# Folding the fourth quarter of the odd layer's weights in the opening instead of in the second attention

## The chip, the cores and the metric

The kernel is one launch on one NeuronCore of a Trainium2 chip. Its metric is the device time in microseconds (us) of that core. The engines named below are PE (TensorE, the matrix engine; PEld is its weight load), DVE (VectorE), ACT (ScalarE), POOL (GpSimd) and SP (SyncE, which here only issues DMA transfers). They run side by side, each works through its own instructions in order, and semaphores make one wait for another.

## The reference: what is computed

One step of a two-layer model on 1024 latent and 256 context tokens of width 1024, all in float32. Layer 0 is attention: mixer A is global, mixer B reads a band of 128 tokens to either side, and both also read the context. Layer 1, the odd layer, mixes by a Fourier transform over positions and over the channels of a group:

```python
def fourier_mix(u):
    b, s, _ = u.shape
    ug = u.astype(jnp.float32).reshape(b, s, C_GROUPS, C_GROUP_DIM)   # 4 groups of 256
    f = jnp.fft.fft2(ug, axes=(1, 3), norm="ortho")
    return jnp.real(f).reshape(b, s, C_WIDTH).astype(u.dtype)

def odd_mix(h, w_in, w_out):
    u, gate = jnp.split(h @ w_in, 2, axis=-1)
    return (fourier_mix(u) * jax.nn.silu(gate)) @ w_out
```

The transform over the channels of a group is linear and follows `h @ w_in` directly, so a kernel may apply it to the weights: for each of the four groups the 1024 x 256 block of `w_in` is multiplied once by a 256 x 256 table of cosines and sines. That product is called the fold here, one group's share of it a quarter.

## The kernel before

Products that need float32 accuracy are mostly made of three cheaper ones: each operand is split into a rounded high part (type fp32r) and the rest, and high*high, high*low and low*high are summed. The fold itself multiplies plain float32.

**The fold.** `fold_load` (L586) brings the table (`fch`, tile `h`, 256 KB) if it isn't there, and the quarter's weights in two transfers of 512 KB (`w<-i_wuT`, L592) into two buffers of zone `w`, which has eight. `fold_piece` (L603) makes a fourth of a quarter: four matrix products into one PSUM bank (`wa`, L609), of which the profile counts two instructions each, then a copy out of PSUM by ACT (L316). A quarter is thus 32 matmul instructions and four ACT copies. Its result goes to DRAM (`wd`, L599) and is read again in the odd layer (L1607), at about 940 to 990 us.

**Where quarters are folded.** Quarters 0 to 2 are folded first of all: the string `PH0` (L32) is the opening's list of steps, and its order is the order in which SP issues the opening's transfers (L709 fixes that order for SP; on the other engines a scheduler orders the instructions). `f0 f1 f2` are the loads, `F00` to `F23` the pieces, whose results wait in pairs in `u` buffers, and `G00` to `G21` the six stores of 512 KB, which stand later in the list. Of the other steps, `x0`, `x1` and `x2` load the tokens, `L0` to `L3` and `A0` to `A3` load and multiply the modulation weights (`ada`), `M` turns such a product into shift and scale (`modt`, then DVE's `modb` and `moda`), `T`, `X`, `Y` transpose and modulate the tokens, and `K`, `R` multiply them by the first projection (`kv0s` to `kv6s`). `ADA_BEHIND` (L59) holds a part of the `ada` products back until a named matmul stands ahead of them; its first entry names quarter 2's last piece.

Quarter 3 is done some 690 us later. Attention runs over units (one query block of 128 tokens, one key/value head, two query heads), and a queue of other matrix work, the filler (L97), is let out between units, by a credit per unit: first the projections of gate, query and key, then `FLATE`'s quarter (four pieces, credit 1.3 each), then the output projection of layer 0 (`oz`, `proj_step` L1387, credit 7.7 a step). Only the first steps of that projection may run inside the attention (`can_run`, L1456), since they need finished rows of all heads; their inputs are brought by POOL and SP, multiplied by POOL (L1284, L1285), and split into high part (ACT, L316) and low part (DVE, L322).

**An attention unit** of mixer B takes from PE scores (`sC` for the context, `sB` for the band), transposes of the probabilities (`pt`, L1108) and the product with the values (`av`, L1114); from DVE the band's mask (L1067), the row maxima (L1023), the low part of the transposed probabilities (L1111) and the sum of two halves (L1125); from ACT the exponentials and the copies of high parts; from SP the load of queries (`q<-qd`, L994) and the store of results.

`EF` (L41) says how many quarters are laid out in DRAM for the opening: for those, each of the two transfers holds all rows of the contraction for one half of the columns, so that two pieces can start after the first one.

```python
EF = 3
ADA_BEHIND = {(0, 0): ("wa", 2, 3), (1, 0): ("xt", 0, 2), (2, 0): ("xt", 0, 4), (2, 16): ("kc", 2, 3)}
FLATE = "f3"
```

Of the kernel before, what the change touches and what calls it, by code (L numbers as in the profile page):

```python
# [9 lines left out]
F32 = mybir.dt.float32  # L10
# [18 lines left out]
WSTEP = ((2, 1, 2), (1, 0, 1))  # L29
ORD_B = (0, 2, 3, 4, 7, 6, 5, 1, 8, 9)  # L30
AT_K, AT_Q, AT_X, NX1, GL = 1, 2, 5, 7, 3
PH0 = """f0 f1 f2 x0 S0 N0 L0 F00 F01 F02 F03 w0 L1 F10 F11 F12 F13 F20 F21 F22 F23 x1 A0 T0 s0 M0 T1 X0 X1 T2 L2 N1 K0 K1  # L32
 A1 T3 M1 L3 X2 X3 K2 K3 Y0 R0 Y1 R1 w1 G00 G01 S1 T4 A2 x2 N2 Y2 T5 M2 R2 G10 G11 G20 G21 X4 Y3 X5 R3
 K4 Y4 K5 A3 T6 Y5 M3 R4 X6 T7 R5 X7 Y6 K6 Y7 K7 R6 R7"""
S1 = """s1 S2 V Z0 Z1 c0 I0 a2 Z2 Z3 c1 I2 a1 q0 P Z4 Z5 I4 a2 P Z6 Z7 I6 a1 q2 P a2 P k8 a2 P a3 P a9 P"""
ADA_Z = (("p", "pt", "q"),) * 4
# [1 line left out]
XZ = ("u", "u", ("p", "pt", "q"))  # L38
E_ML = ("dp", "dp", "d")
E_MF, E_MH, LC0 = "da", "d", "ppd"  # L40
EF = 3  # L41
QPRE, HOLD, AHEAD = 0, 0, 2
PLACE = (
    ((0, 0, 128),), ((128, 0, 128),), ((385, 0, 127), (256, 127, 1)), ((257, 0, 128),), ((769, 1, 127), (512, 0, 1)),
# [11 lines left out]
WARM = 3  # L56
STEP_BEHIND = {(0, 2, 0, 3): ("xt", 2, 3)}
LONG = ((0, 2, 1, 3), "ckt1", "kT00")
ADA_BEHIND = {(0, 0): ("wa", 2, 3), (1, 0): ("xt", 0, 2), (2, 0): ("xt", 0, 4), (2, 16): ("kc", 2, 3)}  # L59
BEHIND = {7: 5}  # L60
ROWS_BEHIND = (9,)
PW1 = "11111"
# [6 lines left out]
FILL_C, NLATE = 2.9, 8  # L69
E_FQ, E_GD = "d", "d"  # L70
ORDER = "qa0 qa1 kb0 qb0 qb1 g0 g1 g2 g3"
FLATE = "f3"
AT_B = "s"
AT_F = (0, 1, 2)
AT_N, AT_Z = (0, 0, 3, 0, 3, 2, 2, 2, 2, 2, 3, 3, 3), ("p", "pt", "q")
# [71 lines left out]
def hybrid_step(ctx: ExitStack, tc: tile.TileContext, I, O):  # L147
# [26 lines left out]
    def drop(*bufs):  # L174
        for b in bufs:
            stamp[0] += 1
            spare[b.zone].append((stamp[0], b.idx))
# [125 lines left out]
    def queue_behind(ins, first):  # L303
        tc.add_manual_dep(
            getattr(ins, "ins", ins), getattr(first, "ins", first).name,
            mybir.DependencyInfo(mybir.DependencyClass.NoSync, mybir.DependencyReason.DATA), reason="order",
        )
# [205 lines left out]
    def ada_mm(ps, j, b, raw, start, stop):  # L513
        return pe.matmul(ps[32 * j : 32 * j + 32, 0:P], csw[:, b, :], raw, start=start, stop=stop)
# [31 lines left out]
    def ada_chunk(kk, raws):  # L546
        ps = bank("g", f"ada{kk}")
        for b in range(8):
            for j in range(4):
                part, i = divmod(j, 2)  # L550
                raw = raws[b // 4 * 2 + part]
                mm = ada_mm(ps, j, b, raw[:, b % 4, i * P : i * P + P], b == 0, b == 7)
                if (kk, 4 * b + j) in ADA_BEHIND:
                    queue_behind(mm, lows[ADA_BEHIND[kk, 4 * b + j]])
        if kk == 1:
# [30 lines left out]
    def fold_load(g):  # L586
# [4 lines left out]
        for i in range(2):  # L591
            sp.dma_start(wu[i].a, I["wuT"][g, i])  # L592
        if g < EF:
            return lambda j, c: wu[c // 512][:, j * 512 + c % 512 :][:, 0:P], wu
# [8 lines left out]
    def fold_piece(g, kb2, wu, first=False):  # L603
# [22 lines left out]
        if kb2 == 3:  # L626
            drop(*wu[1])
            fold["n"] = fold.get("n", 0) + 1
            if fold["n"] in (EF, 4):
                drop(f)  # L630
# [79 lines left out]
    region.__enter__()  # L710
    for op in PH0.split():
        first_step(op)
# [743 lines left out]
    def can_run(i, j):  # L1456
        r = pairs[i][j]

        def fn():
            if sum(len(spare[z]) for z in OB[0]) < NSP or i > EARLY:  # L1460
                return False
            return all(finished.get(t, 99) + SPAN < clock[0] for t in USES[r])
        return fn
# [5 lines left out]
    def load_to(n):  # L1469
        while loaded[0] <= min(n, 9):  # L1470
            proj_load(*steps[loaded[0]])
            loaded[0] += 1
        return 0


    def late_fold(nm):
        def fn():
            ws[nm] = fold_load(int(nm[1]))
            return 0
        return fn  # L1480

    for n, nm in enumerate(FLATE.split()):
        fl_.add(0.0, late_fold(nm))
        if n == 0:
            fl_.add(0.0, lambda: load_to(0), ready=can_run(0, 0))
        for k in range(4):
            fl_.add(FC, lambda k=k, nm=nm: fold_piece(int(nm[1]), k, ws[nm]))
    if not FLATE:
        fl_.add(0.0, lambda: load_to(0), ready=can_run(0, 0))
# [571 lines left out]
```

## Time and profile before

| what | value |
|---|---|
| time before, median of three runs | 1179.93 us (1179.76 to 1182.26) |
| the profiled execution's own time | 1181.93 us |
| its span, first to last instruction | 1180.1 us |
| mean granted TensorE clock | 0.995 |
| PE, PEld, DVE, ACT, POOL busy in the span | 98%, 88%, 70%, 48%, 28% |
| quarters 0 to 2 on PE | 6.3 to 27.2 us |
| quarter 3 on PE | 690.2 to 706.3 us, in four pieces between attention units |

A timeline row reads: start, duration, engine, line, operation, output<-inputs, form, count of merged instructions, and in brackets the engine's idle time just before it with what ended it. A row of windows reads: the window, its length, busy time and count of instructions for PE, PEld, DVE, ACT and POOL, the granted clock, the share of the 16 DMA engines' time, and GB/s. Matmuls are pipelined and their recorded ends are modelled, so that a row of x8 ends later than the next row begins; the distance from start to start is what a matmul costs.

### The profile page before, as it was taken

The page shows a single profiled execution, that of the slowest core. Times are in us where ns is not written, and L with a number is a line of the kernel's source. Part 1 is how long each engine was busy: PE and PEld are TensorE (multiplying, and loading weights), DVE is VectorE, ACT ScalarE, POOL GpSimd, SP SyncE. Part 2 cuts the span into 40 slices and gives each one's busy share as a digit, 9 for nine tenths or more (in the row PEclk, how much of TensorE's full clock was granted, in tenths as well). Part 3 has the DMA queues.
Part 4 walks back from the last instruction along what each step waited for, and adds up shares of the span by engine and source line. Part 5 has one row for each costly group of instructions (what it writes and reads, how often), then busy time and mean ns, then how long its engine had stood idle before and what let it go on. Part 6 is the DMA issues. An engine that isn't in the chain of part 4 may idle for free.

```text
span 1180.1 us, 22034 instructions
## 1 busy us (share of the span) xinstructions
PE 1151.1 (98%) x8120; PEld 1035.5 (88%) x8120; DVE 829.7 (70%) x1996; ACT 570.2 (48%) x1149; POOL 329.8 (28%) x293
## 2 busy tenths in 40 slices
PE   9998999999999999999999989999999999999997
PEld 8797999999999998899989878887777889998886
DVE  3589787877777776678888877776765962468543
ACT  4343466565656655556666674432363234342211
POOL 2345733512222230010110035365221226200001
PEclk9999999999999999999999999999999999999999
DMA  9977412323532232344352587784214426364321
GB/s 368 371 275 256 129 62 68 97 83 101 151 90 79 77 97 85 94 127 117 78 154 78 158 227 211 232 238 162 90 46 143 151 98 181 100 213 146 125 107 54
DMA packets 112592, 168.80 MB, mean 143 GB/s; under 512 B 25946, under 2 KB 63574, under 8 KB 112484
## 3 DMA queue, kind: packets, MB, share of 16 engines
q1 hardware_dynamic: 109972, 158.74, 42.6%
q0 software_dynamic: 2368, 8.39, 2.4%
q8 instruction: 64, 1.05, 0.4%
q14 instruction: 44, 0.36, 0.1%
q10 hardware_dynamic: 144, 0.26, 0.1%
HBM read 123.19 MB, written 44.16 MB: 142 GB/s over the span
## 4 chain that ended last, share of the span: by engine, by line
PE 70%; DMA 13%; DVE 8%; issue 3%; POOL 2%; ACT 2%; SPq 1%; POOLq 0%; DVEq 0%; ACTq 0%
PE of L296 9%; PE av L1114 9%; PE pt L1108 8%; PE ga L296 8%; PE q L296 8%; PE sL L989 5%; PE u L296 5%; PE g1O L296 3%; PE kv L296 3%; PE sC L989 2%; PE g1E L296 2%; PE oz L296 2%; DMA u<-i_x 2%; DMA wd<-u 2%; PE g1c L296 1%
## 5 line engine op out<-in xcount | busy, mean ns | idle before, releaser
L1111 DVE TENSOR_TENSOR pt<-pt,pt 128x512 fp32r<-128x512 f32 (+1 forms) x264 | 170.9, 658 | 40.5 <-ACT pt L316 39.5
L316 ACT ACTIVATE pt<-pt 128x512 fp32r<-128x512 f32 (+1 forms) x265 | 147.5, 576 | 101.8 <-PE pt L1108 56.2
L1114 PE MATMUL av<-pt,u 128*128 128x256 f32 x1008 | 167.5, 290 | 1.4 <-DVE e L1125 0.8
L1108 PE MATMUL pt<-identr,p 128*128 128x128 f32 x1008 | 157.2, 273 | 1.5 <-ACT p L1030 0.8
L296 PE MATMUL q<-w,u 128*128 128x256 f32 x960 | 145.1, 287 | 0.5 <-ACT e L559 0.5
L1114 PEld LDWEIGHTS av<-pt,u 128*128 128x128 f32 x1008 | 139.1, 190 | 5.0 <-DVE e L1125 1.0
L296 PEld LDWEIGHTS q<-w,u 128*128 128x128 f32 x960 | 127.2, 189 | 5.5 <-ACT e L559 0.7
L1030 ACT ACTIVATE p<-p,nm 128x1280 f32<-128x1280 f32 (+1 forms) x80 | 95.4, 1193 | 68.2 <-DVE p L1023 68.0
L1108 PEld LDWEIGHTS pt<-identr,p 128*128 128x128 f32 x1008 | 119.7, 141 | 8.1 <-ACT p L1030 1.0
L296 PE MATMUL ga<-u,w 128*128 128x512 f32 (+1 forms) x576 | 124.4, 360 | 0.8 <-DVE byp L1085 0.5
L296 PEld LDWEIGHTS ga<-u,w 128*128 128x128 f32 x576 | 93.8, 188 | 15.4 <-ACT pt L316 1.2
L322 POOL TENSOR_TENSOR w<-h,w 128x512 fp32r<-128x512 f32 x38 | 50.0, 1331 | 134.6 <-DVE w L318 106.6
L989 PE MATMUL sL<-u,q 128*128 128x512 f32 x256 | 82.3, 409 | 0.0
L1030 ACT ACTIVATE p<-p,NM 128x640 f32<-128x640 f32 (+2 forms) x80 | 59.2, 740 | 31.5 <-DVE p L1023 31.2
L989 PE MATMUL sC<-u,q 128*128 128x256 f32 x320 | 62.1, 294 | 2.3 <-DMA q<-qd 2.0
L1023 DVE TENSOR_SCALAR_CACHE_REDUCE p<-sL 128x512 f32<-128x512 f32 x64 | 43.8, 685 | 22.3 <-PE sL L989 14.0
L1023 DVE TENSOR_SCALAR_CACHE_REDUCE p<-sL,nm 128x512 f32<-128x512 f32 x64 | 47.7, 745 | 13.9 <-PE sL L989 12.8
L296 PE MATMUL oz<-u,w 128*128 128x512 f32 x192 | 56.4, 399 | 0.4 <-DVE e L1125 0.4
L759 POOL TENSOR_TENSOR h<-h,rope 128x512 f32<-128x512 f32 (+1 forms) x18 | 21.6, 1199 | 121.4 <-ACT h L842 79.2
L989 PEld LDWEIGHTS sC<-u,q 128*128 128x128 f32 x320 | 48.8, 189 | 5.9 <-issue 2.6
L322 POOL TENSOR_TENSOR u<-h,u 128x512 fp32r<-128x512 f32 x16 | 21.0, 1323 | 109.1 <-ACT u L316 81.2
L296 PE MATMUL of<-u,u 128*128 128x512 f32 x150 | 48.2, 393 | 0.0
(735 smaller groups left out, 2590.7 us busy)
## 6 DMA issues: line engine op xcount, KB each, us to landing
q<-qd SPq DMA_DIRECT2D x80, 256.0 KB
h<-i_w_in SPq DMA_DIRECT2D x40, 256.0 KB
h<-i_w_out SPq DMA_DIRECT2D x32, 256.0 KB
p<-i_ada_s SPq DMA_DIRECT2D x11, 512.0 KB
qd<-pt SPq DMA_DIRECT2D x20, 256.0 KB
qd<-q SPq DMA_DIRECT2D x18, 256.0 KB
w<-i_wuT SPq DMA_DIRECT2D x8, 512.0 KB
u<-i_x SPq DMA_DIRECT2D x8, 512.0 KB
```

Source lines behind the costliest of these rows:

```text
L296: last = pe.matmul(out, a, b, start=i == 0, stop=i == n - 1)
L316: return act.activation(out, in_, AF.Copy)
L322: return pick("lo" + lc, lc).tensor_sub(dst_l, src, dst_h)
L759: pick("rope", XE["rope"]).tensor_mul(t1.rearrange("p t h (b c) -> p t (h b) c", b=2), y.rearrange("p t h (b c) -> p t (h b) c", b=2), cb)
L989: pe.matmul(ps, q_at(q, s, hc), keys, start=s == 0, stop=s == 1)
L1023: dve.tensor_scalar(p[i][:, end[i] : end[i] + n], ps, sign, last[i], op0=ALU.mult, op1=ALU.min, accum_out=c)
L1030: act.activation(p[i][:, 0 : end[i]], p[i][:, 0 : end[i]], AF.Exp, bias=last[i], scale=-1.0, accum_out=SU[:, t, hd + i, 0:1],)
L1108: pe.transpose(tp[:, jj * 256 + i * P : jj * 256 + i * P + P], p[i][:, off : off + P], ident)
L1111: dve.tensor_sub(pt[:, 1, 0:n], tp[:, 0:n], pt[:, 0, 0:n])
L1114: pe.matmul(acc, vv, pt[:, s, jj * 256 : jj * 256 + 256], start=c + jj + s == 0, stop=c + jj == nt - 1 and s == 1,)
```

## The change

Quarter 3 joins the opening. Its loads stand behind those of quarter 2, its four pieces behind quarter 2's, and its two stores behind quarter 2's. The load of the first projection's weights (`w0`, with `L1`) moves behind quarter 1's pieces, since four quarters fill the eight `w` buffers. The first modulation products now stand behind quarter 3's last piece. The filler loses quarter 3, its two loads and the second load of the table.

```diff
-PH0 = """f0 f1 f2 x0 S0 N0 L0 F00 F01 F02 F03 w0 L1 F10 F11 F12 F13 F20 F21 F22 F23 x1 A0 T0 s0 M0 T1 X0 X1 T2 L2 N1 K0 K1
- A1 T3 M1 L3 X2 X3 K2 K3 Y0 R0 Y1 R1 w1 G00 G01 S1 T4 A2 x2 N2 Y2 T5 M2 R2 G10 G11 G20 G21 X4 Y3 X5 R3
+PH0 = """f0 f1 f2 f3 x0 S0 N0 L0 F00 F01 F02 F03 F10 F11 F12 F13 w0 L1 F20 F21 F22 F23 F30 F31 F32 F33 x1 A0 T0 s0 M0 T1 X0 X1 T2 L2 N1 K0 K1
+ A1 T3 M1 L3 X2 X3 K2 K3 Y0 R0 Y1 R1 w1 G00 G01 S1 T4 A2 x2 N2 Y2 T5 M2 R2 G10 G11 G20 G21 G30 G31 X4 Y3 X5 R3
...
-EF = 3
+EF = 4
...
-ADA_BEHIND = {(0, 0): ("wa", 2, 3), (1, 0): ("xt", 0, 2), (2, 0): ("xt", 0, 4), (2, 16): ("kc", 2, 3)}
+ADA_BEHIND = {(0, 0): ("wa", 3, 3), (1, 0): ("xt", 0, 2), (2, 0): ("xt", 0, 4), (2, 16): ("kc", 2, 3)}
...
-FLATE = "f3"
+FLATE = ""
```

The scheduler then orders the engines anew. SP's queue from its first transfer on, before the change (`h<-i_fch` is the table, `w` the folded weights, `u<-i_x` the tokens):

```order
L589 DMA h_135<-i_fch 128x512
L592 DMA w_137<-i_wuT 128x1024
L592 DMA w_138<-i_wuT 128x1024
L592 DMA w_141<-i_wuT 128x1024
L592 DMA w_142<-i_wuT 128x1024
L592 DMA w_145<-i_wuT 128x1024
L592 DMA w_146<-i_wuT 128x1024
L450 DMA u_149<-i_x 128x1024
```

And of the change:

```order
L589 DMA h_135<-i_fch 128x512
L592 DMA w_137<-i_wuT 128x1024
L592 DMA w_138<-i_wuT 128x1024
L592 DMA w_141<-i_wuT 128x1024
L592 DMA w_142<-i_wuT 128x1024
L592 DMA w_145<-i_wuT 128x1024
L592 DMA w_146<-i_wuT 128x1024
L592 DMA w_149<-i_wuT 128x1024
L592 DMA w_150<-i_wuT 128x1024
L450 DMA u_153<-i_x 128x1024
```

Two transfers of 512 KB have come in ahead of the tokens and of everything behind them.

The second place is DVE in the second attention, the rows that end with the low part of the first output projection's input (`w<-u,w`, L322), without which that projection can't go beyond its first products. In names such as `sC_20` and `sB_300` the first figure (2 or 3) tells mixer B's key/value head, the second the pair of query heads, a third the head of the pair; before the change:

```order
L1023 TENSOR_SCALAR p_9496,NM<-sC_20_9497,nsink 128x256
L1081 TENSOR_REDUCE tot_9687<-SU 128x16
L1082 TENSOR_SCALAR tot_9687<-tot_9687 128x16
L1023 TENSOR_SCALAR p_9640,NM<-sC_21_9641,nsink 128x256
L1083 RECIPROCAL tot_9687<-tot_9687 128x16
L1111 TENSOR_TENSOR pt_9516<-pt_300_9511,pt_9516 128x512
L1085 COPY byp_9693<-tot_9687 128x16
L322 TENSOR_TENSOR w_9318<-u_9308,w_9317 128x1024
```

And of the change:

```order
L1125 TENSOR_TENSOR e_9445<-av_20_9431,e_9444 64x256
L1111 TENSOR_TENSOR pt_9522<-pt_302_9517,pt_9522 128x512
L1067 SCALAR_TENSOR_TENSOR p_9770<-sB_300_9778,maskf 128x384
L1067 SCALAR_TENSOR_TENSOR p_9770<-sB_301_9783,maskf 128x384
L1023 TENSOR_SCALAR p_9770,nm_301_9769<-sC_30_9771,nsink 128x256
L1081 TENSOR_REDUCE tot_9681<-SU 128x16
L1023 TENSOR_SCALAR p_9770,NM<-p_9770,nm_300_9768 128x384
L1125 TENSOR_TENSOR e_9485<-av_21_9471,e_9484 64x256
L1111 TENSOR_TENSOR pt_9532<-pt_304_9529,pt_9532 128x256
L1023 TENSOR_SCALAR p_9770,NM<-p_9770,nm_301_9769 128x384
L1082 TENSOR_SCALAR tot_9681<-tot_9681 128x16
L322 TENSOR_TENSOR w_9344<-u_9334,w_9343 128x1024
```

The next unit's masks and maxima (`sB_300`, `sB_301`, `sC_30`) now stand ahead of that low part; before they stood behind it. Counted from the last row of the gate projections (L878) up to and with the low part, DVE has 31 rows before and 41 now: six more of L1023, two more each of L1067, L1111 and L1125, and two of the small rows on `tot` fewer.

The third place is PE at the same point, the rows up to the first output projection (`oz`). Before the change, where `wa` are matmuls of quarter 3's last piece:

```order
L609 MATMUL wa_9402<-h_9298,w_9300 128x256
L609 MATMUL wa_9402<-h_9298,w_9301 128x256
L989 MATMUL sC_20_9497<-u_4487,q_9432 128x256 x2
L989 MATMUL sC_30_9704<-u_7091,q_9506 128x256 x2
L989 MATMUL sC_21_9641<-u_4487,q_9432 128x256 x2
L1108 MATMUL pt_310_9651<-identr,p_9456 128x128 x4
L1114 MATMUL av_21_9477<-pt_9483,u_4487 128x256 x4
L296 MATMUL oz_9564<-u_8516,w_9317 128x512
```

And of the change:

```order
L989 MATMUL sC_31_9815<-u_7123,q_9500 128x256 x2
L1061 MATMUL sB_310_9822<-u_7121,q_9500 128x384 x2
L1061 MATMUL sB_311_9827<-u_7121,q_9500 128x384 x2
L296 MATMUL oz_9558<-u_8548,w_9343 128x512
L296 MATMUL oz_9558<-u_8549,w_9343 128x512
L1114 MATMUL av_30_9504<-pt_9510,u_7123 128x256 x4
L1114 MATMUL av_30_9504<-pt_9522,u_7122 128x256 x4
L1114 MATMUL av_30_9504<-pt_9532,u_7122 128x256 x2
L1108 MATMUL pt_314_9669<-identr,p_9450 128x128 x2
L296 MATMUL oz_9558<-u_8548,w_9344 128x512
```

No `wa` is left there. Up to the third `oz` product, the first one that needs the low part, PE now has 8 more of `sB`, 4 more of `sC`, 6 more of `pt` and 10 more of `av` than it had before up to the first `oz`.

## The prediction

> **What bounds the kernel now.** I begin with the page's busy row and the slices of PE and of its granted clock.
>
> ```profile
> PE 1151.1 (98%) x8120; PEld 1035.5 (88%) x8120; DVE 829.7 (70%) x1996; ACT 570.2 (48%) x1149; POOL 329.8 (28%) x293
> PE   9998999999999999999999989999999999999997
> ```
>
> PE is the bound over the whole, and the change takes no matmul away: 32 of them go from one place to another. So the time moves only by what PE waits, or runs slowly, at the old and the new place. The windows view shows both places.
>
> ```profile
> 30.00:40.00 10.00, 7.77 (x108) 6.64 (x107) 5.42 (x17) 7.45 (x13) 3.09 (x3) 0.98 1.03 407
> 40.00:50.00 10.00, 10.00 (x110) 8.50 (x109) 5.56 (x9) 1.45 (x2) 4.61 (x3) 0.84 1.05 402
> 690.00:708.40 18.40, 16.16 (x105) 14.79 (x106) 16.07 (x50) 14.66 (x35) 8.59 (x9) 1.00 0.96 271
> 750.00:760.00 10.00, 8.49 (x39) 7.27 (x40) 9.66 (x27) 7.48 (x20) 0.72 (x1) 0.83 0.54 167
> ```
>
> The opening has a hole in PE (7.77 of 10 us) followed by a granted clock of 0.84, with the DMA engines full (share 1.03). The stretch with quarter 3, 690 to 708.4, is the one to look at twice: DVE is busy 16.07 of 18.40 us there and none of that is the fold's, whose copies run on ACT. Quarter 3 fills PE time that DVE would largely leave empty.
>
> **The opening.** The timeline gives the quarter's price and what PE waits for behind it.
>
> ```profile
> 6.33 20.88 PE L609 MATMUL wa<-h,w 128*128 128x256 f32 x96
> 12.48 0.33 SPq L542 DMA_DIRECT2D p<-i_ada  x1
> 13.77 0.33 SPq L542 DMA_DIRECT2D pt<-i_ada  x1
> 34.16 1.06 ACT L459 ACTIVATE h<-u 128x1024 bf16<-128x1024 f32 x1
> 36.11 0.27 PE L566 MATMUL modt<-identr,e 128*128 128x128 f32 x1
> 36.39 1.42 DVE L465 TENSOR_SCALAR u<-u,n11ry 128x1024 f32<-128x1024 f32 x2 [0.88 <-POOL n11ry L275]
> 37.98 0.16 DVE L532 TENSOR_TENSOR moda<-moda,gT 128x4 f32<-128x4 f32 x1
> 38.09 0.41 PE L471 MATMUL xt<-identr,u 128*128 128x128 f32 x2 [1.71 <-DVE moda L531]
> 39.02 0.50 PE L576 MATMUL kv0s<-w,u 128*128 128x256 f32 x2 [0.52 <-ACT u L484]
> ```
>
> 96 matmuls in 20.88 us are 0.2175 us each, so quarter 3 adds 32 x 0.2175 = 6.96 us of PE ahead of the first `ada` product. SP issues one 512 KB transfer per 13.77 - 12.48 = 1.29 us there, so everything behind the two new loads comes 2.6 us later. PE comes 7.0 us later, hence it no longer waits for what the queue brings: the 1.71 us at 38.09 ended when DVE's `moda` was made, behind the normalising of tokens (L465) that hangs on ACT's squares at 34.16 and so on the load of `x1`. That chain moves by 2.6 us, PE's arrival by 7.0. The 0.52 us at 39.02 is the same chain's next step. Both are covered: -2.2 us. The clock row at 40 to 50 shows 0.84: 10 x 0.16 = 1.6 us of PE work lost, right behind these two gaps. Without the gaps I take the loss as gone. The opening costs +6.96 - 1.71 - 0.52 - 1.6 = **+3.1 us**.
>
> Here a rule bears on the sum. TensorE: Matmul & The Clock Gate, in the Trainium skill, says under Why this matters for your kernels that the clock falls to half after PE idles for a window of about 3.4 us and advises no gaps over about 3 us. The gaps here were 1.71 and 0.52 us and the clock fell all the same, so the trace is stricter than that advice. By the rule alone these gaps wouldn't be the cause, the 1.6 us would stay, and the opening would cost +4.7.
>
> The bounds: +7.0 if nothing is covered. Below, waits further on could absorb the rest:
>
> ```profile
> PE ad L514 <- DMA p<-i_ada_s: 2.2, 2, 1.5
> PE ad L514 <- DMA q<-i_ada_s: 1.0, 1, 1.0
> 49.90 7.00 SPq L599 DMA_DIRECT2D wd<-u  x4
> 76.97 0.65 PE L514 MATMUL ad<-p,e 128*32 128x128 f32 x16
> ```
>
> The first two rows (waits from 0 to 130 us) sum to 3.2 us, so 0 is the low end. I take +3.1, since these transfers are issued late and move along with PE's work. The other queue effect is the two added stores: four took SP 7.00 us, so two take 3.5, and transfers behind them come 2.6 + 3.5 = 6.1 us later. They are the `ada_s` loads, issued from 57 us and first used at 76.97; PE's own shift and that distance hide it. The buffers that the stores release are taken up later in the list, and I price them at nothing.
>
> **The second attention.** Rows of DVE and PE around quarter 3:
>
> ```profile
> 690.12 0.69 DVE L1111 TENSOR_TENSOR pt<-pt,pt 128x512 fp32r<-128x512 f32 x1
> 690.22 1.97 PE L609 MATMUL wa<-h,w 128*128 128x256 f32 x8 [0.39 <-ACT pt L316]
> 692.06 0.47 DVE L1023 TENSOR_SCALAR_CACHE_REDUCE p<-sC,nsink 128x256 f32<-128x256 f32 x1
> 692.46 0.54 DVE L1067 SCALAR_TENSOR_TENSOR p<-sB,maskf 128x384 f32<-128x384 f32 x1
> 693.05 0.51 PE L1061 MATMUL sB<-u,q 128*128 128x384 f32 x2
> 693.41 0.52 PE L1114 MATMUL av<-pt,u 128*128 128x256 f32 x3
> 693.53 0.60 DVE L1023 TENSOR_SCALAR_CACHE_REDUCE p<-p,nm 128x384 f32<-128x384 f32 x1
> 696.21 0.40 DVE L1125 TENSOR_TENSOR e<-av,e 64x256 f32<-64x256 f32 x1
> 697.45 0.60 PE L1108 MATMUL pt<-identr,p 128*128 128x128 f32 x4
> 697.81 1.19 PE L1114 MATMUL av<-pt,u 128*128 128x256 f32 x8
> 698.84 0.38 PE L1108 MATMUL pt<-identr,p 128*128 128x128 f32 x2
> 703.02 0.48 DVE L1023 TENSOR_SCALAR_CACHE_REDUCE p<-sC,nsink 128x256 f32<-128x256 f32 x1 [1.79 <-PE sC L989]
> 704.41 1.89 PE L609 MATMUL wa<-h,w 128*128 128x256 f32 x8
> 705.41 1.23 DVE L322 TENSOR_TENSOR w<-u,w 128x1024 fp32r<-128x1024 f32 x1 [0.22 <-ACT w L316]
> 708.46 0.87 PE L296 MATMUL oz<-u,w 128*128 128x512 f32 x3
> ```
>
> Before, DVE runs 31 rows from the end of L878 at 690.12 to the end of the low part (705.41 + 1.23 = 706.64): 16.5 us, with 1.79 + 0.22 = 2.0 idle. The change puts 41 rows there. By these durations the ten are 6 x 0.53 (L1023, 0.47 to 0.60) + 2 x 0.69 + 2 x 0.54 + 2 x 0.40, less some 0.4 for two small rows: 6.0 us. Each row starts some 0.07 us before the last one ends (690.12 + 0.69 against 690.73 is typical), 0.8 over twelve: 5.2. So DVE needs 19.7 us if its idle time goes (the 1.79 was a load of queries that shared the DMA engines with the fold's traffic) and 21.7 if not. I take the middle, 20.7: the low part ends at 710.8 on the old clock of that place and the main run of `oz` starts there, against 708.46: +2.3 us. Though 7 us of matmuls are gone, the projection starts later.
>
> But PE then has less left. It has done 10 more `av` ((698.84 - 697.81) / 8 = 0.13 each), 6 `pt` ((697.81 - 697.45) / 4 = 0.09), 8 `sB` ((693.41 - 693.05) / 2 = 0.18) and 4 `sC`, which I price like `av`: 1.3 + 0.5 + 1.4 + 0.5 = 3.7 us. Net -1.4, between -2.4 and -0.4.
>
> Behind it stands a second stall:
>
> ```profile
> 750.35 0.28 PE L1088 MATMUL tt<-identr,byp 128*16 128x128 f32 x1 [0.85 <-DVE pt L1111]
> 750.95 0.33 PE L1108 MATMUL pt<-identr,p 128*128 128x128 f32 x1 [0.32 <-DVE ssp L1418]
> 752.11 0.55 PE L1108 MATMUL pt<-identr,p 128*128 128x128 f32 x3 [0.84 <-ACT p L1030]
> ```
>
> These 0.85 + 0.32 + 0.84 = 2.0 us, with the clock of 0.83 behind them (1.7 us), come from DVE being behind. With 5.2 us of its rows done earlier they may go or stay: between -3.7 and 0, and I take half, -1.9. The place gives -1.4 - 1.9 = **-3.3 us**, between -6.1 and -0.4.
>
> From there on the same work follows in a slightly other order, which the windows from 850 to 1050 bound:
>
> ```profile
> sum 200.00, PE 195.50 PEld 172.30 DVE 119.13 ACT 79.12 POOL 59.78; mean PE 48.87 PEld 43.07 DVE 29.78 ACT 19.78 POOL 14.95
> ```
>
> PE idles 4.5 of 200 us there. I take 0 for it, within 1.5 either way.
>
> **The sum.** +3.1 - 3.3 = -0.2 us on the profiled execution's 1181.93, so 1181.7. That execution stands 2.0 above the median of 1179.93, hence 1179.7 for the median. A measurement of this kernel can tell about 0.2%, 2.4 us, from no change; the forecast lies within it.
>
> **Rivals.**
>
> *The stretch gives all back (faster).* If DVE runs without idling and the stall at 750 with its clock drop goes, the place gives -6.1, and with the opening at +3.1 the time falls by 3.0 to 1176.9. For it: the DMA engines at 0.96 in that stretch lose the quarter's traffic. Against: the 41 rows in the order.
>
> *The emptied stretch drops the clock (slower).* PE's 16.16 busy us lose the fold's (1.97 + 3 x 1.89 = 7.6) and gain 3.7: 12.3 us of work in 20.7. The two clock losses above followed stretches with little PE work, so here the clock may stay at half. Then PE needs 24.6 us where DVE needs 20.7: 3.9 us more, in all 1183.6. It decides once PE's work at half clock exceeds DVE's 20.7. Against it: from 690 to 708 PE waits 2 us for queries already and the clock reads 1.00. The same page of the Trainium skill says, under PE-mode transpose, that transposes don't count as PE work for the clock; the `pt` rows here are transposes, which speaks for this rival, and no row here shows it by itself.
>
> *The opening is not covered (slower).* If PE meets its waits at 38 and 39 us again and the clock drops again, the opening costs +7.0 and the sum is +3.7, 1183.6. It decides once the `x1` chain moves by as much as PE does, 7.0 us instead of 2.6.
>
> That quarter 3 is folded twice or not at all is excluded by the order of instructions.
>
> **Chances and range.** Forecast (within 0.2%) 0.44; the stretch gives all back 0.30; clock 0.12; opening uncovered 0.14. So faster 0.30, same 0.44, slower 0.26. The forecast's own range is 1177.6 to 1182.3. For 8 in 10 I go below the first rival by a part of the opening's low end, to 1174.5, and above the slower two by a little, to 1184.5.
>
> **What would show it.** Opening: the `modt` of the second `ada` product followed by no wait of 1.7 us, the clock at 1.00 from 40 to 50 us, and the `ad` products at 76.97 some 3 us later. Attention: PE waiting for DVE between the last `ga` and the first `oz`, DVE almost without idle time there, and the third `oz` about 20 us behind the last L878. The prediction is wrong if `oz` follows within 17 us, if the clock reads below 0.9 in that stretch, or if the 1.71 us wait stays.

## The result and the profile after

| | before | after |
|---|---|---|
| time, median of four runs each | 1180.84 us (1179.76 to 1182.26) | 1194.49 us (1192.64 to 1195.88) |
| ratio | | 1.0105, 95% interval 1.0078 to 1.0132 |
| profiled execution's own time | 1181.93 us | 1195.64 us |
| its span | 1180.1 us | 1193.6 us |

The change makes the kernel 13.7 us slower, far more than the 0.2% (2.4 us) that a measurement can tell. The forecast of no change was wrong, and so was its range, which ended at 1184.5. (The ratio of the two medians alone is 1.0116, a little above the ratio given but within its interval.)

The page of the changed kernel, rows of busy time and slices:

```profile
PE 1156.5 (97%) x8120; PEld 1039.5 (87%) x8120; DVE 838.8 (70%) x1996; ACT 569.3 (48%) x1149; POOL 331.3 (28%) x293
PE   9999999999999999999999979999999998999997
```

The instruction counts are those of before. PE is busy 5.4 us longer (1156.5 against 1151.1) and idle 8.1 us longer (span less busy: 37.1 against 29.0). Slices hide this; the view of windows finds the places. First the changed kernel (window, its length, busy us and instructions of PE, PEld, DVE, ACT, POOL, granted clock, DMA share, GB/s):

```profile
30.00:40.00 10.00, 10.00 (x108) 8.49 (x106) 1.98 (x6) 5.17 (x11) 1.88 (x2) 1.00 1.00 371
40.00:50.00 10.00, 9.46 (x146) 8.07 (x145) 8.92 (x19) 6.38 (x11) 4.65 (x4) 1.00 1.02 399
65.00:80.00 15.00, 14.51 (x123) 14.10 (x122) 12.04 (x23) 8.34 (x15) 6.90 (x6) 1.00 0.95 351
612.00:625.00 13.00, 10.70 (x61) 9.45 (x59) 10.10 (x30) 9.02 (x19) 2.59 (x2) 0.87 0.73 204
690.00:712.00 22.00, 15.93 (x118) 14.84 (x116) 14.84 (x46) 11.55 (x28) 7.18 (x9) 0.89 0.87 230
973.00:1013.00 40.00, 34.26 (x266) 31.38 (x265) 9.72 (x30) 13.71 (x32) 17.75 (x22) 0.96 0.48 143
```

The same view of the kernel before, for the windows that the prediction didn't show:

```profile
65.00:80.00 15.00, 14.95 (x161) 14.38 (x161) 12.75 (x31) 5.73 (x10) 6.63 (x6) 1.00 0.54 200
612.00:625.00 13.00, 13.00 (x80) 11.51 (x79) 11.92 (x37) 9.60 (x22) 1.29 (x1) 1.00 0.58 154
690.00:712.00 22.00, 19.75 (x121) 17.73 (x122) 17.27 (x53) 15.91 (x39) 11.85 (x14) 1.00 0.92 262
973.00:1013.00 40.00, 38.58 (x365) 36.76 (x363) 11.03 (x42) 16.74 (x44) 22.02 (x25) 1.00 0.60 178
```

In the opening the hole and the lost clock at 30 to 50 are gone, but the DMA engines are at 0.95 instead of 0.54 from 65 to 80. At 612 and from 690 PE idles and loses clock, and in the Fourier mixing, at 973, PE gets through 266 instead of 365 instructions. Laid side by side by the start of the same matmul (the n-th with the same output), PE stands behind the profiled execution of before as follows. The marks are the 29th `kv4s` (66.1 us before), the `ga` at 565, the last `ga` (687), the last `oz` of layer 0 (851), the first `u` of the Fourier stage (973), the `u` at 1012 and the last `of` (1173). The first four rows fold quarter 3 late, as before. Each row is one profile. Ahead of each mark PE has done the same matmuls in all of them, except those of quarter 3. The last `modt`, at 65.3 us, would not do as a mark: the changed kernel is only 3.1 us late there, but runs 15 other matmuls behind it (3 `q`, 6 `kv0s`, 6 `kv2s`) that stood ahead of it before.

| us behind, at | 66 | 565 | 687 | 851 | 973 | 1012 | 1173 | median of the runs |
|---|---|---|---|---|---|---|---|---|
| before again (e4) | -0.7 | 1.0 | 0.6 | -0.9 | -0.9 | -0.1 | -0.1 | 1181.85, one run |
| two more stores (e8) | -0.1 | 5.3 | 4.2 | 2.6 | 2.1 | 2.2 | 2.2 | 1183.86 |
| other turn of buffers (e13) | -0.7 | -0.2 | -0.4 | -0.5 | -0.5 | 5.3 | 5.4 | 1186.72 |
| a `u` buffer, before (e14) | -0.1 | 0.7 | 0.1 | -1.1 | -1.1 | 0.6 | 0.4 | 1181.10 |
| **after** | 5.9 | 5.9 | 7.3 | 7.1 | 7.2 | 13.5 | 13.7 | 1194.49 |
| folded twice (e1) | 5.7 | 6.3 | 6.7 | 13.8 | 12.2 | 14.4 | 14.3 | 1196.07 |
| empty quarter kept (e2) | 5.9 | 7.2 | 7.3 | 12.3 | 10.6 | 12.1 | 12.0 | 1194.52 |
| late part alone (e3) | -0.2 | 2.6 | 1.0 | -2.0 | -2.3 | 2.6 | 2.5 | 1187.81 |
| no gate loads (e6) | 4.0 | 5.1 | 7.3 | 17.6 | 15.9 | 21.6 | 21.8 | 1203.89 |
| a `u` buffer (e7) | 5.3 | 5.8 | 5.6 | 5.6 | 5.6 | 7.0 | 7.1 | 1188.89 |
| stores from POOL (e9) | 5.0 | 6.0 | 8.2 | 7.8 | 7.9 | 16.6 | 16.8 | 1196.15 |
| queries ahead (e11) | 5.6 | 7.5 | 9.2 | 9.6 | 8.9 | 19.9 | 20.2 | 1198.55 |
| queue's turn (e12) | 7.2 | 7.2 | 9.2 | 10.9 | 10.7 | 16.3 | 16.5 | 1194.43 |
| no stores of quarter 3 (e15) | 4.0 | 3.0 | 4.9 | 5.6 | 5.0 | 11.4 | 11.6 | 1193.11 |

In its one repeat (e4) the kernel before stands within 1 us of its first profile at these marks; the times of its runs beside the experiments lay between 1172.87 and 1185.44. For the changed kernel the row splits into 5.9 (opening) + 1.4 (565 to 687) - 0.2 (attention and projection) + 0.1 + 6.3 (973 to 1012) + 0.2 = 13.7 us.

### The profile page after: what moved, and what is told of

It reads as the page before. It is cut to its first block, busy times and chain, and to the rows that moved or that the text cites. A ratio compares the mean times of both kernels' runs of the same rounds, so it can differ in the third digit from the quotient of the medians.

```text
span 1193.6 us, 22024 instructions
## 1 busy us (share of the span) xinstructions
PE 1156.5 (97%) x8120; PEld 1039.5 (87%) x8120; DVE 838.8 (70%) x1996; ACT 569.3 (48%) x1149; POOL 331.3 (28%) x293
## 4 chain that ended last, share of the span: by engine, by line
PE 79%; DVE 7%; DMA 6%; issue 3%; ACT 2%; POOL 1%; SPq 1%; POOLq 0%; DVEq 0%; ACTq 0%
PE av L1114 9%; PE of L296 9%; PE pt L1108 9%; PE ga L296 9%; PE q L296 8%; PE sL L989 5%; PE u L296 4%; PE oz L296 3%; PE g1O L296 3%; PE sC L989 3%; PE kv L296 3%; PE wa L609 2%; PE g1E L296 2%; PE g1c L296 1%; PE sB L1061 1%
## 5 line engine op out<-in xcount | busy, mean ns | idle before, releaser
L1111 DVE TENSOR_TENSOR pt<-pt,pt 128x512 fp32r<-128x512 f32 (+1 forms) x264 | 170.6, 658 | 39.7 <-ACT pt L316 38.9
L322 POOL TENSOR_TENSOR w<-h,w 128x512 fp32r<-128x512 f32 x38 | 50.5, 1346 | 132.2 <-DVE w L318 104.8
L296 PE MATMUL oz<-u,w 128*128 128x512 f32 x256 | 65.4, 398 | 1.9 <-DVE h L1308 1.2
L1023 DVE TENSOR_SCALAR_CACHE_REDUCE p<-sL 128x512 f32<-128x512 f32 x64 | 43.9, 686 | 23.5 <-PE sL L989 14.7
L296 PEld LDWEIGHTS oz<-u,w 128*128 128x128 f32 x256 | 47.2, 188 | 13.1 <-DVE h L1308 1.5
L1023 DVE TENSOR_SCALAR_CACHE_REDUCE p<-sL,nm 128x512 f32<-128x512 f32 x64 | 47.7, 746 | 13.0 <-PE sL L989 11.9
L322 POOL TENSOR_TENSOR u<-h,u 128x512 fp32r<-128x512 f32 x22 | 31.0, 1419 | 89.7 <-ACT u L316 89.4
```

What stands on the lines that cost most here:

```text
L296: last = pe.matmul(out, a, b, start=i == 0, stop=i == n - 1)
L322: return pick("lo" + lc, lc).tensor_sub(dst_l, src, dst_h)
L1023: dve.tensor_scalar(p[i][:, end[i] : end[i] + n], ps, sign, last[i], op0=ALU.mult, op1=ALU.min, accum_out=c)
L1111: dve.tensor_sub(pt[:, 1, 0:n], tp[:, 0:n], pt[:, 0, 0:n])
```

## The experiments

**e1, e2: is it the missing quarter?** Both start from the changed kernel. e1 folds quarter 3 at the old place as well. e2 takes and gives back the old place's buffers and lets the same credits pass, with empty pieces.

```diff
 e1
-FLATE = ""
+FLATE = "f3"
 e2
-FLATE = ""
+FLATE = "f3"
-            ws[nm] = fold_load(int(nm[1]))
+            ws[nm] = [take(z, (P, n)) for z, n in (("h", 512), ("w", 1024), ("w", 1024))]
-            fl_.add(FC, lambda k=k, nm=nm: fold_piece(int(nm[1]), k, ws[nm]))
+            fl_.add(FC, lambda k=k, nm=nm: drop(take("h", (P, 512)), *(ws[nm] if k == 3 else ())))
```

> Quarter 3 is folded twice: in the opening as after the change, and again in the second attention as before it (the same numbers are stored twice). Theory A (three separate costs: the opening some +6 us, a late weight load with a clock loss near 618 us +3 us, and the buffers in the Fourier stage near 975 to 1005 us +6.4 us, while the emptied stretch near 700 us gives nothing net): the opening's cost alone remains here, 1187 us, or 1190 us if the loss near 618 us comes along. Theory B (the opening costs the predicted +3.1 us and all the rest, some 10 us, comes from the stretch that the change empties): 1184 us.

> The changed kernel, but the filler keeps an empty quarter: at the old place the same buffers (one of zone h for the table, two of zone w, one of zone h per piece) are taken and given back with the same credits, and nothing is loaded, multiplied, copied or stored there. From the odd layer on every tile then lies in the buffers that it had before the change. Theory A (the 6.4 us lost between 975 and 1005 us come from the other buffers and the other order of loads that follows): 1188 us, no new loss between 975 and 1005 us. Theory B (they come from the shifted times, whatever the buffers): 1194 us.

e1: 1196.07 us (ratio 1.0139, interval 1.0110 to 1.0169); e2: 1194.52 us (1.0122, 1.0084 to 1.0160). Neither theory's time came in e1; e2's time is theory B's, but its loss lies where theory A had it. From 687 to 851 e1 loses 7.1 us and e2 5.0: 32 matmuls more or less at the late place are worth about 2 us, not 7. (That both lose there, though e1 does what the kernel before does, goes with the scheduler's order, which it made anew: PE's rows there differ from both kernels'.) What is new: with the old place's buffers booked, the loss from 973 to 1012 shrinks to 2.2 (e1) and 1.5 us (e2) from 6.3. The Fourier stage is sensitive to which buffers the filler took, 280 us earlier.

**e3, e8: the two halves apart.** Both start from the kernel before. e8 stores quarter 2's result twice, so that the opening has six stores but no more matmuls. e3 does the same and also leaves the late fold out; quarter 2 stands in for quarter 3.

```diff
 e3 alone
-FLATE = "f3"
+FLATE = ""
 e3 and e8
-            fold_put(i // 10, i % 10 * 512, e.a)
+            [fold_put(q, i % 10 * 512, e.a) for q in ((2, 3) if i // 10 == 2 else (i // 10,))]
```

> The kernel of before without quarter 3 in the second attention, and without it in the opening: quarter 3's place in DRAM gets quarter 2's result by two more stores, so 32 matmuls, three loads and four copies are left out. From the odd layer on the buffers and the order are those of the changed kernel. Theory A: the emptied stretch gives nothing net although 7 us of matmuls are gone, and the Fourier stage costs 6.4 us: 1187 us. Theory B (the Fourier stage's loss comes with the opening, the stretch gives the predicted 3.3 us): 1177.5 us.

> The kernel of before with the two stores of quarter 2 made twice (into quarter 3's place, which the late fold then overwrites): the opening's added stores alone. From some 350 us on every engine has the order of before. Theory A (what is lost in the second attention and in the Fourier stage comes from the new order and buffers there): 1180 to 1183 us, no clock loss near 700 and 985 us beyond those of before. Theory B (the late stretches lose because everything ahead of them has moved): above 1186 us.

e8: 1183.86 us (ratio 1.0036, interval 1.0012 to 1.0059); e3: 1187.81 us (1.0075, 1.0055 to 1.0095; its profile, at 1184.37, is the fastest of its nine runs, so its row above flatters it). The two differ in the late quarter alone, and the kernel without its 32 matmuls is the slower one by 4.0 us; 4.9 us are lost again from 973 to 1012, against 0.1 in e8. Theory A held in e3; e8's time lies just above theory A's range, far from theory B's.

**e4: the kernel before, once more**, for the spread.

> The kernel of before, unchanged, for a second profile of it. Theory A (when PE's clock first reads 1.00 is chance, so that 1.95 us of the 9.4 us by which the first ada products came later aren't the change's): the clock reads half up to some time between 5.5 and 11 us, other than the 5.56 us of the first profile in about half of such looks, and the fold ends up to 2.4 us later than in it. Theory B (the change causes it): full clock from 5.6 us again. Time 1177 to 1184 us by either.

1181.85 us. Its full clock starts later than in the first profile, and its first `oz` 3.5 us later against `ga` (0.6 behind at 687, 4.1 at 708); by 851 nothing of either is left.

**e7, e13, e14: the turn of the buffers.** The Fourier stage takes eight raw buffers for the 129-column parts of the stored quarters, each from whichever zone's buffer has been free the longest: in turn pt q w w q pt q w before, pt q w q pt q w q after. e7 gives the changed kernel the old turn with a `u` buffer in the fourth place, e13 gives the kernel before the new turn, e14 gives it e7's.

```diff
 e7 from after, e14 from before (with "f3" for "")
-FLATE = ""
+FLATE, RAWZ = "", deque(("pt", "q", "w", "u", "q", "pt", "q", "w"))
 e13 from before
-FLATE = "f3"
+FLATE, RAWZ = "f3", deque(("pt", "q", "w", "q", "pt", "q", "w", "q"))
 all three
-                    raw = take(("p", "pt", "q", "w"), (P, 2, width))
+                    raw = take(RAWZ.popleft(), (P, 2, width))
```

> The changed kernel with one edit in the Fourier stage: the fourth load of the folded weights goes into a buffer of zone u instead of q, where it had to wait until the second load's products were done, so that it is issued with the third. Nothing differs ahead of some 945 us. Theory A (the loss of 6.4 us between 975 and 1005 us comes from this buffer): 2 us or less are lost there, 1189 to 1190 us. Theory B (it comes from the transfers' own duration, 6.3 us instead of 5.1 for the third load, and from ACT's order): 1193 to 1194 us.

> The kernel before, quarter 3 still folded late, but the eight 129-column loads of the odd layer's weights take their buffers in the zones that they take after the change (pt q w q pt q w q in place of pt q w w q pt q w). Theory A (the loss of 6.3 us between 973 and 1012 us in the changed kernel comes from the turn of the buffers alone): PE falls behind the kernel before by 4 to 7 us in that stage and by nothing ahead of it, and the time is 1184 to 1187. Theory B (the turn costs only because the changed kernel arrives there otherwise, with its DMA traffic and its attention shifted): less than 1.5 us lost in that stage, time 1178 to 1181.

> The kernel before with the fourth of the eight 129-column loads in a buffer of zone u instead of w, the edit that took about 5 us of loss from the changed kernel. Theory A (in the kernel before that load is early enough): within 1.5 us of the kernel before, 1178 to 1181, and PE between 973 and 1012 us moves by less than 1.5. Theory B (it is late there too: before the change a u product waits 1.3 us at 982): PE gains 1.5 to 3 us in that stage, time 1176.5 to 1178, faster than both kernels.

e7: 1188.89 us (ratio 1.0087, interval 1.0055 to 1.0119). e13: 1186.72 us (1.0063, 1.0040 to 1.0085). e14: 1181.10 us (1.0019, 0.9999 to 1.0039). Theory A held in e7 and e13; e14 lies at its edge (1.7 us lost in the stage) and far from theory B's gain. With the new turn and nothing else changed, the kernel before loses 5.8 us between 973 and 1012; without it the changed kernel loses 1.4 there instead of 6.3. The timeline shows how. SP's later 129-column loads of the kernel before (the two rows left out are of 128 columns, into `h`):

```profile
980.55 0.36 SPq L1607 DMA_DIRECT2D w<-wd  x1
981.58 0.36 SPq L1607 DMA_DIRECT2D q<-wd  x1
...
991.55 0.37 SPq L1607 DMA_DIRECT2D pt<-wd  x1
992.01 0.46 SPq L1607 DMA_DIRECT2D q<-wd  x1
992.58 0.45 SPq L1607 DMA_DIRECT2D w<-wd  x1
```

The same loads in the changed kernel:

```profile
988.74 0.36 SPq L1607 DMA_DIRECT2D q<-wd  x1
...
1002.19 0.37 SPq L1607 DMA_DIRECT2D q<-wd  x1
1002.62 0.50 SPq L1607 DMA_DIRECT2D pt<-wd  x1
1003.22 0.45 SPq L1607 DMA_DIRECT2D q<-wd  x1
1003.71 0.51 SPq L1607 DMA_DIRECT2D w<-wd  x1
```

Two loads went out by 982 before, one by 989 now; the fifth load stands in a `pt` buffer that comes free only at about 1002, 21 us after its old time (a `q` buffer, at 981.58), where PE is 7 us late. In e13 as many loads are out by 982 as before, but one of them is the seventh, in the second `w` buffer of the turn; the fifth goes out 10 us after its old time:

```profile
980.01 0.36 SPq L1607 DMA_DIRECT2D w<-wd  x1
991.52 0.49 SPq L1607 DMA_DIRECT2D pt<-wd  x1
```

What PE then waits for, in the changed kernel and, behind it, in e13:

```profile
991.33 0.62 PE L296 MATMUL u<-u,u 128*128 128x258 f32 x3 [2.49 <-ACT u L316]
993.14 0.36 PE L296 MATMUL u<-u,w 128*128 128x258 f32 x1 [1.19 <-DVE h L1565]
1006.88 0.63 PE L296 MATMUL u<-u,w 128*128 128x258 f32 x3 [1.07 <-ACT u L316]
1008.62 2.43 PE L296 MATMUL u<-u,w 128*128 128x258 f32 x18 [0.98 <-POOL u L322]
```

```profile
996.16 0.63 PE L296 MATMUL u<-u,w 128*128 128x258 f32 x3 [1.48 <-ACT u L316]
998.93 1.13 PE L296 MATMUL u<-u,w 128*128 128x258 f32 x6 [2.03 <-DVE nyr L1816]
```

ACT and POOL split what the loads bring, and PE waits for them; the two DVE rows named in the brackets stand behind ACT, for which DVE waited 8.98 and 0.91 us just before. The waits are not the same rows in both kernels, only the stage and roughly the sum agree. Over all profiles it goes with the turn: the seven with the new one (after, e3, e6, e9, e12, e13, e15) lose 4.9 to 8.7 us from 973 to 1012, the seven with the old one or the `u` buffer (before, e1, e2, e4, e7, e8, e14) 0.0 to 2.2. e7's row of the same stretch, with the clock whole again:

```profile
973.00:1013.00 40.00, 37.26 (x335) 34.75 (x334) 9.98 (x32) 14.86 (x37) 20.96 (x23) 1.00 0.48 141
```

e14 beats nothing: before the change that load is early enough.

**e9, e15: the opening's stores.** From the changed kernel, e9 issues quarter 3's two stores on POOL. e15 leaves them out of the opening; queries copied within DRAM, from 205 to 221 us, fill their place, so two outputs aren't the reference's.

```diff
 e9
-        sp.dma_start(wd[g // 2, :, r0 // P : r0 // P + n, g % 2, :], src)
+        (pool if g == 3 else sp).dma_start(wd[g // 2, :, r0 // P : r0 // P + n, g % 2, :], src)
 e15
-            fold_put(i // 10, i % 10 * 512, e.a)
+            i // 10 == 3 or fold_put(i // 10, i % 10 * 512, e.a)
...
+    for k in range(4):
+        sp.dma_start(wd[1, :, 2 * k : 2 * k + 2, 1, :], qd[k, 1].rearrange("p (a c) -> p a c", a=2))
```

> The changed kernel with quarter 3's two stores issued by POOL instead of SP, so that SP's queue loses the 3.8 us which two more stores take there (10.79 us for six instead of 7.00 for four). From some 300 us on the order is that of the changed kernel. Theory A (the opening costs more than the forecast 3.1 us because the loads behind the stores, ada_s and the queries, come later): PE's work from 250 to 600 us lies 3 to 4 us behind the first profile of before instead of 6.0, and the time is 1190 to 1192 us. Theory B (it is the fold's own 7 us that come through): still 6 us behind, 1194 us.

> The changed kernel without the two stores of quarter 3 in the opening (its four pieces stay; what is read in its place later are queries, copied within DRAM at some 130 to 170 us, so two outputs are not the reference's). Theory A (PE's 32 matmuls cost the opening 3 us, as they show up to 65 us, and the two added stores the 3 us behind that, through the modulation weights of the second list and what waits for them): PE between 300 and 600 us stands 2 to 4 us behind the kernel before instead of 6, time 1190 to 1192.5. Theory B (the stores are of no account, all 6 us come from the matmuls and the loads): 5 to 7 us behind there, time 1193.5 to 1196.

e9: 1196.15 us (ratio 1.0142, interval 1.0100 to 1.0184), 6.0 us behind at 565 like the changed kernel: its theory A failed. e15: 1193.11 us (1.0119, 1.0094 to 1.0144), 3.0 us behind at 565: theory A held for the place, not for the time, which fell by 1.4 us (medians; 2.1 at 1173 in the profiles). The changed kernel's profile is not its fair neighbour, since its full clock starts early (5.43 us against 10.77, last section). e6 has the changed kernel's opening and an early start (5.32): both stand 4.0 us behind at 66, then 5.1 (e6) and 3.0 (e15) at 565, so the two stores cost 2.1 us there. That may be too low, as e15 is only 0.7 behind at 215 and then waits 2.0 us for queries, behind its copies, which the changed kernel doesn't. The view of waits from 65 to 160 us (us in total, times, longest), of the changed kernel and then of e15:

```profile
PE kT L735 <- POOL h L766: 2.1, 1, 2.1
PE ad L514 <- DMA q<-i_ada_s: 1.5, 1, 1.5
PE sL L989 <- DMA q<-qd: 1.0, 1, 1.0
```

```profile
PE ad L514 <- DMA p<-i_ada_s: 1.9, 3, 1.1
```

Of what loads bring, only `ad`'s operands are late in e15. And SP's part, in the changed kernel and in e9, where POOL issued the other two stores from 33 to 36 us:

```profile
54.06 10.79 SPq L599 DMA_DIRECT2D wd<-u  x6
64.98 1.20 SPq L909 DMA_DIRECT2D p<-i_ada_s  x1
```

```profile
54.55 6.22 SPq L599 DMA_DIRECT2D wd<-u  x4
60.87 3.08 SPq L909 DMA_DIRECT2D p<-i_ada_s  x1
```

e9 gives SP its 4 us back, and the loss stays. So it isn't SP's issuing; the stores' 1 MB in engines that are full anyway fits both runs, though no run varies the bytes alone: each edit of the stores also gives PE another order, from some 85 to 420 us in e15. The Trainium skill says the like under Issuing engines are not separate DMA queues (DMA: Bandwidth & Descriptors): transfers share the same 16 engines whichever engine starts them. e9 agrees, with 6.0 us against 5.9.

**e6, e11: the queries at 709.** From the changed kernel, e6 drops two loads of the gate (512 KB each) for the projection's first rows (another operand stands in), e11 loads queries up to two blocks ahead.

```diff
 e6
-            ld.dma_start(gl.a, gate[r])
+            r in pairs[0] or ld.dma_start(gl.a, gate[r])
-            pick("pm", XE["pm"]).tensor_mul(gl.a, gl.a, rl.a)
+            pick("pm", XE["pm"]).tensor_mul(gl.a, (ol if r in pairs[0] else gl).a, rl.a)
 e11
-        q = take("q", (P, 2, 512))
+        q = take("q" if spare["q"] else "w", (P, 2, 512))
-            nx = next((u[:2] for u in units[n:] if u[:2] != (t, g)), None)
-            if pr == QPRE and nx is not None and nx not in qs and ("q", nx[0] // 2 * 2, nx[1]) in fl_.done:
-                qs[nx] = load_q(*nx)
+            for nx in list(dict.fromkeys(u[:2] for u in units[n:] if u[:2] != (t, g)))[: 2 if g > 1 else 1]:
+                if pr == QPRE and nx not in qs and ("q", nx[0] // 2 * 2, nx[1]) in fl_.done and (spare["q"] or len(spare["w"]) > 2):
+                    qs[nx] = load_q(*nx)
```

> The changed kernel with 1 MB less traffic in the emptied stretch: the gate's load (512 KB) is left out for the first two rows of the output projection, whose product is made with the attention's result in the gate's place; POOL's work stays. Theory A (the emptied stretch is bound by transfers: PE's sC waits 5.7 us at 703 to 709 us for queries that stand behind the projection's inputs): that wait falls below 2.5 us, the clock loses at most one window of 3.4 us there, and the time is 1187 to 1190 us. Theory B (DVE's 41 rows bound the stretch): the first oz comes at the same distance and the time is 1194 us.

> The changed kernel, with the queries of mixer B loaded up to two query blocks ahead instead of one where a buffer (q, or w if three are free) is there. The order is that of the changed kernel up to the emptied stretch. Theory A (the stretch gives nothing because PE's sC then waits 5.7 us for a load of queries and the clock halves for 6.8 us): that wait falls below 1.5 us, the clock loses at most 3.4 us there, the first oz comes 4 us earlier, and the time falls to 1188 to 1190 us. Theory B (DVE's rows bound the stretch): PE waits for DVE instead and the time stays within 2 us of 1194 us.

e6: 1203.89 us (ratio 1.0205, interval 1.0167 to 1.0243): the scheduler let the `oz` rows out in another order and the place lost 10 us, so neither theory was tested. e11: 1198.55 us (1.0166, 1.0123 to 1.0208), outside both theories' times. Its timeline:

```profile
701.88 0.58 SPq L994 DMA_DIRECT2D q<-qd  x1
711.67 1.20 PE L989 MATMUL sC<-u,q 128*128 128x256 f32 x4 [4.87 <-DMA q<-qd]
```

The load that PE waits for still goes out 10 us ahead of its use, as in the changed kernel, so the edit didn't bring it forward and theory A wasn't tested. It loses 11.0 us from 973 to 1012, with yet another turn of the buffers, since its queries take `w` buffers too.

**e12: the queue's turn.** Four loads of 4 KB more in the changed kernel's opening shift every later transfer on SP's queue by four places, in case that delays the load at 607. The trace lists SP's transfers in one queue (q1) and gives them eight semaphores, mostly in turn; the change moved them on by four, and in e12 the two loads at 608 have again the two that they had before.

```diff
-    sink = cp.tile([P, 8], F32, name="sink")
+    sink, *more = [cp.tile([P, 8], F32, name=f"sink{k}") for k in range(5)]
-            sp.dma_start(sink, I["sink"].partition_broadcast(P))
+            [sp.dma_start(d, I["sink"].partition_broadcast(P)) for d in [sink, *more]]
```

> The changed kernel with four more loads of 4 KB in the opening, which nothing uses. [...] The order is that of the changed kernel but for a few rows ahead of 130 us. Theory A (the loss near 618 us, 1.5 to 3 us, comes from queues that now take other transfers' turns): the two loads of weights issued at 606.9 us take SP 2.4 us again instead of 3.6 to 4.4, nothing is lost near 618 us, and the time is 1191 to 1193 us. Theory B (the queue number is of no account): 3.6 us or more, 1194 us.

1194.43 us (ratio 1.0126, interval 1.0081 to 1.0171): theory A failed, the two loads at that place take SP 4.38 us all the same.

## Why the prediction was wrong, step by step

**The opening up to 66 us: the mechanism right, the size too small.** "The opening costs +6.96 - 1.71 - 0.52 - 1.6 = +3.1 us." It cost 5.9. The changed kernel's timeline, against 27.15 us before for the first `ada`, 36.11 and 65.30 for the second and the last `modt`, and 76.97 for `ad`:

```profile
36.52 0.30 PE L514 MATMUL ada<-p,e 128*32 128x128 f32 x2
43.53 0.33 PE L566 MATMUL modt<-identr,e 128*128 128x128 f32 x1 [0.26 <-ACT e L559]
68.44 0.27 PE L566 MATMUL modt<-identr,e 128*128 128x128 f32 x1
81.95 0.65 PE L514 MATMUL ad<-p,e 128*32 128x128 f32 x16
```

The waits of 1.71 and 0.52 are gone and the clock reads 1.00. PE is 9.4 us late at the first `ada`, 7.4 at the second `modt` and 5.9 at 66 us, so it made up 3.5 of the 3.8 us that the sum deducts. (The `ad` come 5.0 us later, not some 3.) What the sum lacked is the 9.4 in place of 6.96: the full clock started at 10.77 us here, at 5.56 in the first profile of before (last section). e6 and e15, with the same opening and the full clock from 5.32 and 5.43, are 6.8 and 7.0 us late at the first `ada` and 4.0 at 66. The kernel before pays nothing for a late start, because its waits take it up. Its repeat e4, with the full clock from 9.73, is 2.0 us late at the first `ada` and 0.7 ahead at 66; the row of the 1.71 us wait and the window with the lost clock read there:

```profile
38.74 0.41 PE L471 MATMUL xt<-identr,u 128*128 128x128 f32 x2 [0.41 <-DVE moda L531]
40.00:50.00 10.00, 10.00 (x122) 8.32 (x120) 6.78 (x11) 1.72 (x3) 4.62 (x3) 1.00 1.04 401
```

So the sum deducted waits and a lost clock that only an early start leaves. Of the six profiles with the opening of before, the clock falls at 40 us in the two with an early start (before; e8, waits of 1.16 and 0.82) and in none of the four with a late one (e3, e4, e13, e14, waits of 0.41 and 0.51). By the rule of the Trainium skill that the prediction weighed (TensorE: Matmul & The Clock Gate, Why this matters for your kernels) the drop had another cause and would have stayed, for 4.7 us; the traces don't agree, since the drop went with the waits, in the changed kernel and in those four.

**The added stores: the step that failed in the opening.** "PE's own shift and that distance hide it", and of their buffers, "I price them at nothing". From 66 to 565 us the profiles with all the changed kernel's stores fall back by 0.0 to 1.9 us and e15 gains 1.0; like for like (e6 and e15) the two stores cost 2.1. On the kernel before they cost about 2 us (e3 is 2.6 behind at 565, e4, e13 and e14 from -0.2 to 1.0) to 5.3 (e8, which has e3's order of PE up to there). The mis-sized term is thus some 2 to 5 us instead of 0. I counted SP's 6.1 us but not the engines, which are busy from 65 to 80 us by 0.54 before, 0.76 in e8, 0.66 in e15 and 0.95 in the changed kernel; and the loads that I took as covered by distance are waited for (`ada_s` 1.5 us, queries 1.0). That the full engines make them late is argued. The wait of `kT` ends with POOL, and what delays POOL wasn't followed.

**The second attention: -3.3 predicted, -0.2 found, and the reason was wrong.** The main run of `oz` was to start 20.7 us behind the last L878 row; its first product, the third `oz`, comes 24.9 us behind it. The wrong step is the wait in "19.7 us if its idle time goes", with "1.79 was a load of queries that shared the DMA engines with the fold's traffic" and so would go. The changed kernel's timeline:

```profile
699.23 0.60 SPq L994 DMA_DIRECT2D q<-qd  x1
709.20 1.19 PE L989 MATMUL sC<-u,q 128*128 128x256 f32 x4 [5.71 <-DMA od<-e]
720.85 1.43 PE L296 MATMUL oz<-u,w 128*128 128x512 f32 x5 [0.40 <-DVE w L322]
```

The wait for queries did not go, it grew: the two before (2.0 us in all) hung on a load of queries too, and PE had matmuls of the fold to do meanwhile. The releaser named in the bracket is only the event nearest in time; the queries issued at 699.23 have landed at 709.07. DMA stays at 0.87 from 690 to 712, though the fold's load isn't there. "PE then has less left ... 3.7 us" gave nothing either. From the `oz` run to 851 us PE takes 137.2 us against 142.5 before, but the repeat e4, which loses no clock at 753, takes 137.4 with all its matmuls. Across the kernels with the late quarter this place (687 to 851) changes by 0 (before), -1.5, -1.6, -0.1 and -1.2 us, without it by -0.2, 0.0, -0.4, 1.7, 0.7 and -3.0 (after, e7, e9, e12, e15, e3; e1, e2, e6 and e11, whose order there is another, left out): the means are -0.9 and -0.2. PE's work isn't what ends this place, so taking 7 us of it away is worth nothing. In the repeat e4 a late load ends it with the fold in place, too:

```profile
693.59 0.63 ACT L316 ACTIVATE u<-h 128x512 fp32r<-128x512 f32 x1 [6.77 <-DMA h<-i_w_out]
695.10 3.07 PE L609 MATMUL wa<-h,w 128*128 128x256 f32 x8 [4.18 <-ACT pt L316]
```

The same two waits are 7.09 and 4.96 us in e13, 5.89 and 3.75 in e14; the first profile, from which the prediction was made, has 0.39 for the second. That full DMA engines make these loads late is argued, not shown, since e6 and e11 both missed.

**Rival B (a clock lost in the emptied stretch): seen, not shown to be the cause.** The clock does read 0.89 from 690 to 712, below the 0.9 that the prediction named as a sign of being wrong. But the kernel before loses it there as well, with the late quarter in place: for 3.41 us in e4 and e14 and for 6.83 us, as long as the changed kernel, in e13. e4's row:

```profile
690.00:712.00 22.00, 17.74 (x105) 16.16 (x105) 15.32 (x46) 14.87 (x35) 9.20 (x9) 0.92 0.87 255
```

**"From there on the same work ... within 1.5 either way": the costliest step.** It lost 6.3 us. The windows of before said how little PE idles there, and I took that for safety; it says only that the loads just came in time. Two `w` buffers that the filler no longer takes change which buffer has been free the longest 280 us later, and with it the load that comes late. e13 and e7 show it from both sides. No order around the change tells it; the loads' rows in the order of the odd layer (their zones) would have.

**Between 565 and 687, 1.4 us: a lost clock; why the load behind it is late stays open.** PE waits 2.1 us for DVE at 618, behind a weight load whose second issue is late, and the clock halves for 3.41 us, 1.7 us of work:

```profile
606.87 3.95 SPq L1170 DMA_DIRECT2D h<-i_w_out  x2
616.77 0.69 DVE L322 TENSOR_TENSOR u<-h,u 128x512 fp32r<-128x512 f32 x1 [2.73 <-ACT u L316]
617.99 0.73 PE L1061 MATMUL sB<-u,q 128*128 128x384 f32 x2 [2.12 <-DVE p L1067]
```

Before, the two issues took 2.46 us. e7, e1 and e2 wait 1.9, 2.4 and 2.2 us at the same place, keep their clock, and the stretch costs them -0.2, 0.4 and 0.1; e7's order of PE is the changed kernel's up to there. e6, e9, e11, e12 and e15 lose the clock and 1.7 to 2.2 us. So the load is late each time and the lost clock is what costs. What delays the load isn't the queue's turn (e12), nor SP's stores (e9); what it is wasn't found.

No kernel tried here measurably beats the one before.

## What to carry to other kernels

A piece of work that fills holes is worth the holes, not its length: before moving it, ask what ends the stretch without it. A wait or a lost clock that one profile shows may be missing in the next (1.71 against 0.41 us here), so take the price of a hole from a repeat as well. Where buffers are handed out by the longest free, a change of who takes one can make a load late hundreds of microseconds on, so compare the zones of every later load, not just the order around the edit. And count a transfer by the busy share of the DMA engines where it lands too, not only by the queue that issues it: e9 freed SP and gained nothing.

## What was not expected of the hardware

The time at which the full clock starts is left to chance. The view of windows from 5 to 11 us, in the first profile of the kernel before, in its repeat and in the changed kernel:

```profile
5.00:11.00 6.00, 6.00 (x31) 5.05 (x30) 0.00 (x0) 1.20 (x2) 0.00 (x0) 1.00 1.01 360
```

```profile
5.00:11.00 6.00, 6.00 (x22) 4.81 (x21) 0.00 (x0) 0.60 (x1) 0.00 (x0) 1.00 1.00 371
```

```profile
5.00:11.00 6.00, 6.00 (x20) 4.67 (x19) 0.00 (x0) 0.47 (x1) 0.00 (x0) 1.00 0.96 380
```

The same stream of matmuls advances by 31, 22 and 20 rows, at a clock that the view gives as 1.00; the trace's record has it full from 5.56, 9.73 and 10.77 us on. Over the 15 profiles it starts between 4.2 and 5.8 us in five and between 9.4 and 10.9 in ten. A difference of 2 to 3 us at the first `ada` is thus no effect of an edit. In the kernel before it is gone by 66 us; the changed kernel, which has no waits left there to take it up, keeps 1.3 to 1.9 us of it (4.0 in e6 and e15, 5.3 to 5.9 in e1, e2, e7, e11 and the changed kernel). Later the changed kernel's clock halves for whole periods of 3.41 us (once at 618, two in a row at 707, once at 994), each during or right behind waits of PE of about 2 to 6 us.
